# A two-layer attention trunk on one core: the columns and vectors of v's scales made by ScalarE instead of VectorE

## The chip, the core and the metric

The kernel runs on one core of a Trainium2 chip. The core has five engines that are used here: TensorE (PE in the profile; its weight loads are PEld), VectorE (DVE), ScalarE (ACT), GpSimd (POOL) and SyncE (SP), which issues all DMAs. Every engine works through its own list of instructions in order; an instruction that waits holds up everything behind it on its engine. The metric is the device time of one execution in microseconds (us), lower is better. The kernel before took 1829.58 us (median of 3 runs, 1827.2 to 1830.59).

## What is computed

The reference is a trunk of two layers over a sequence of 1024 rows of 1024 numbers, float32, one batch. Each layer adds to x a gated mixer's output through an output matrix:

```python
for i in range(DEPTH):                       # DEPTH = 2
    h = rms_norm(x, norm_g[i])
    if i % 2 == 0:
        o, gate = fox_mixer(h, ...)          # causal attention with a forget gate
        w_out = fox_w_out[0]
    else:
        o, gate = dsw_mixer(h, cos, sin, ...)  # three dilated sliding windows, mixed by softmax
        w_out = dsw_w_out[0]
    x = x + (o * silu(gate)) @ w_out
```

The FoX mixer projects h to q, k, v, gate and a forget logit (16 heads of 64), normalizes q and k, and attends causally with a decay. The dilated mixer (DSW) projects h to q, k, v of three groups (windows 128, 512, 2048 with dilations 1, 4, 16) and a gate, normalizes q and k and rotates a part of them, attends in each group within its window, and mixes the three groups by their log sums.

## The kernel before, in words

**Rounds.** The projections of both layers are worked off in rounds. A round is a pair of heads (FoX: 8 rounds) or a pair of heads and a group (DSW: 24 rounds, first the 8 of group 0, then groups 2 and 1 in turn for each pair of heads). In a round, `project` (line 313) multiplies eight tiles of 128 rows with the round's weights, 384 columns (128 each of k, q, v) and 8 slabs of 128 rows of the weights. Each product is made of three matmuls: activations and weights are both split into a high part and a remainder (`xh`, `xl`; `w[:, 0]`, `w[:, 1]`), and high times high, high times remainder and remainder times high are summed.

**Weights.** A round's weights are loaded as four tiles `raw` of two slabs each (line 253, two buffers), and each slab is split: ACT casts the high part (line 289), then GpSimd or, for slabs 4 and 6, DVE takes the remainder (line 291). `bound` (line 258) takes the largest absolute value of the columns of v on DVE, and `scale` (lines 270 to 281) makes from it a power of two, `vs`, by which v is scaled so that it fits in float16 as two parts. These steps belong to the next round and are put in during the present one by `Flow`, a table of slots that is advanced by four ticks a tile (the offsets in `CFG`: `wload`, `wbound`, `wscale`, `wsplit`).

**v and its scale.** At the start of a round two small instructions make what v needs: `v_tile` (line 462) writes `vs` into column 128 of each of the 8 x 2 blocks of the tile `vt` (128x16 numbers; that column is the row sum's column in the product of probabilities and v), and lines 743 (FoX) and 996 (DSW) multiply the 8 row factors of the norm with `vs` to `vsr` (128x8). Both are `tensor_scalar` instructions of DVE. For each tile, lines 388 (ACT) and 389 (DVE) then write v times `vsr` into `vt` as a high part and a remainder.

**q and k.** For each tile DVE multiplies q and k with the gains out of the projection's PSUM tile `pj` (line 378, to `u`), ACT squares them (383); for each two tiles DVE sums the squares (396, 398), ACT and DVE make the inverse root inside `pj` (416 to 420), DVE applies it to `u` (422, which reads `pj` last), ACT casts a high part to `hl` (424), GpSimd takes the remainder (425), DVE copies the two k blocks in exchanged order (426), and SP transposes `hl` by DMA to `qk_t` (430). In the DSW rounds GpSimd rotates a part of `u` before that (410 to 413). There are three buffers of `pj`, so TensorE cannot begin a tile before the tile three earlier has been read for the last time.

**Attention.** Scores are matmuls of `qk_t` tiles (450); DVE adds the mask or decay and takes the minimum (658, 906), ACT makes the exponentials (492, 907) and casts them (495, 911), GpSimd takes the remainder (498, 912), SP transposes by DMA to `ptt` (499, 913), and TensorE multiplies with `vt` (506 to 508). In group 1, GpSimd also weighs the three groups (936 to 940) and DVE combines them (947 to 955).

**Order.** TensorE's order is as the program is written. The lists of the other engines are ordered by a scheduler at build time, from its own estimate of how long each instruction takes; so moving an instruction to another engine can also change the order around it.

Of the kernel before, what the change touches and what calls it, by code (L numbers as in the profile page):

```python
# [16 lines left out]
AF = mybir.ActivationFunctionType  # L17
ALU = mybir.AluOpType
# [4 lines left out]
P = 128  # L23
# [3 lines left out]
NT = S // P  # L27
# [24 lines left out]
def tile_cols(g, t):  # L52


    if g < 2:
        return slice(t * P, (t + 1) * P, 1)
    a = 2 * P * (t % 4) + t // 4
    return slice(a, a + 2 * 127 + 1, 2)
# [24 lines left out]
def trunk(ctx, tc, ins, out, cfg):  # L83
    nc = tc.nc
# [31 lines left out]
    def lay(shape, dtype, name, tag):  # L116
        return layer["pool"].tile(shape, dtype, name=name, tag=tag, bufs=layer["bufs"][tag])
# [187 lines left out]
    def part(src, i, layer=0):  # L305
        return Weights(src[i], src[i].shape[2], None, layer)

    def project(w, cols):
        n = w.n
        ps = under["ps"] = ps_pj.tile([P, 512], F32, name="pj", tag="pj")  # L310
        for k in range(KT):
            for i, (a, j) in enumerate(((xh, 0), (xh, 1), (xl, 0))):
                nc.tensor.matmul(ps[:, :n], a[:, k, cols], w.slabs[k][:, j, :n], start=(k == 0 and i == 0), stop=(k == KT - 1 and i == 2))  # L313
            if k % 2:
                flow.tick()
        return ps
# [142 lines left out]

    def v_tile(vs):  # L460
        vt = lay([P, NT, 2, 129], F16, name="vt", tag="vt")
        nc.vector.tensor_scalar(vt[:, :, :, 128], vs.unsqueeze(2).broadcast_to([P, NT, 2]), 1.0, None, ALU.mult)  # L462
        return vt

    def gates(src, w, nxt, rows, before=None, after=None):
# [48 lines left out]
    rx = const.tile([P, 3, NT], F32, name="rx")  # L514
# [33 lines left out]
    w = part(w_fgate, 0)  # L548
# [72 lines left out]
    def load_bc(hp, h, es=(0, 1)):  # L621
        for e in es:
            bcs[hp, e, h] = lay([P, 512], F32, name="bc", tag="ga")
            nc.sync.dma_start(bcs[hp, e, h], c_d[2 * hp + e, h * 512 : (h + 1) * 512].partition_broadcast(P))
# [103 lines left out]
    def fox_weights(hp):  # L728
        return Weights(w_fox[hp], 384, slice(256, 384), 0)

    w = gates(w_fgate, w, lambda: fox_weights(0), rx, x_ready, forget_logits)
    for hp in range(NHP):
        w2 = (fox_weights(hp + 1) if hp + 1 < NHP else part(w_fo, 0)).ahead()
        s0 = flow.now
        if hp == 0:
            load_bc(0, 0)
        for h, e, slot in cfg["bc"]:
            if hp + 1 - h < NHP:
                flow.at(s0 + slot, lambda n=hp + 1 - h, h=h, e=e: load_bc(n, h, (e,)))
        kts = []  # L740
        vt = v_tile(w.vs)
        vsr = sm.tile([P, NT], F32, name="vsr", tag="vsr")
        nc.vector.tensor_scalar(vsr, rx[:, 0], w.vs, None, ALU.mult)
        for t in range(NT):
            ps = project(w, tile_cols(0, t))
            if t % 2 == 0:
                hd = heads_begin()
            heads_tile(ps, 0, t, hd, vt, vsr[:, t : t + 1], rx[:, 2, t - 1 : t + 1])
            if t % 2:
                with tc.high_priority(cfg["ph_"]):  # L750

                    turn = heads_pair(0, t - 1, hd)
                    flow.at(flow.now + (6 if hp < NHP - 1 else 4), lambda turn=turn, kts=kts: kts.append(turn()))
                for i in range(2):

                    tt = t - 1 + i
                    fox_tile(hp, tt, kts, vt, s0 + (cfg["due"][tt] if hp < NHP - 1 else 4 * tt + 18))
            if hp == NHP - 1:

                a = max(flow.now + 1, s0 + cfg["due"][t] - 4 * NT + cfg["lpf"] + 9)  # L760
                turn_y(t, 0, [(flow.now + 1, flow.now + 8), (a, a + 7)])
        w = w2
# [4 lines left out]
    rx2 = const.tile([P, 3, 3 * NT], F32, name="rx2")  # L767
# [62 lines left out]
    for h in range(len(PARTS)):  # L830
# [17 lines left out]
        w = w2  # L848
# [26 lines left out]
    w = gates(w_gate, w, lambda: dsw_weights(0), rx2, switch)  # L875
# [116 lines left out]
    for ci, (hp, g) in enumerate(order):  # L992
        w2 = (dsw_weights(ci + 1) if ci + 1 < len(order) else part(w_do, 0)).ahead()
        vt = v_tile(w.vs)
        vsr = sm.tile([P, NT], F32, name="vsr", tag="vsr")
        nc.vector.tensor_scalar(vsr, rx2[:, 0, g * NT : (g + 1) * NT], w.vs, None, ALU.mult)
        qks = [None]
        for t in range(NT):
            if ci == NHP - 1:
                reload_x(t)  # L1000
            ps = project(w, tile_cols(g, t))

            LSD, LPD = cfg["lsd"][max(0, ci - len(order) + 3)]
            if t % 2 == 0:
                hd = heads_begin()
            f = g * NT + t
            heads_tile(ps, g + 1, t, hd, vt, vsr[:, t : t + 1], rx2[:, 2, f - 1 : f + 1])
            if t % 2 == 0:
                continue
            t0 = t - 1  # L1010
            with tc.high_priority(cfg["ph_"]):
                qks = [qks[-1], heads_pair(g + 1, t0, hd)()]
            if g != 1:

                def done(og, ob, g=g, hp=hp, t0=t0):
                    nc.scalar.copy(og[:, :, :, : HD + 1], ob[:, : N2 * (HD + 1)].rearrange("p (i e d) -> p i e d", i=2, e=2))
                    rows = og_d[g // 2, hp].rearrange("(i p) d -> i p d" if g == 0 else "(p i) d -> i p d", p=P)
                    nc.sync.dma_start(rows[t0 : t0 + 2].rearrange("i p d -> p i d"), og.rearrange("p i e d -> p i (e d)"))
                    written.update(((hp, g, t0), (hp, g, t0 + 1)))

                dsw_pair(g, t0, qks, vt, done, lambda: lay([P, 2, 2, 66], F32, name="og", tag="og"), LSD, LPD)
            else:
                cmb = {}

                def get(cmb=cmb):
                    cmb[0] = lay([P, 3, CB, 2, 66], F32, name="cmb", tag="cmb")
                    return cmb[0][:, 0]

                def done(dst, ob, hp=hp, t=t, cmb=cmb):
                    if hp == NHP - 1:  # L1030
                        combine(hp, t, cmb, ob)
                    else:
                        flow.at(flow.now + 1, lambda: combine(hp, t, cmb, ob))

                dsw_pair(g, t0, qks, vt, done, get, LSD, LPD)
                flow.at(flow.now + LSD + 2, lambda hp=hp, t0=t0, cmb=cmb: load_cmb(hp, t0, cmb))
                flow.at(flow.now + LSD + LPD - 5, lambda cmb=cmb: weigh(cmb))
                if hp == NHP - 1:
                    for i in range(2):
                        turn_y(t0 + i, 1, [(flow.now + a + 2 * i, flow.now + b + 2 * i) for a, b in cfg["ty2"]])  # L1040
        w = w2
# [8 lines left out]
    for h in range(len(PARTS)):  # L1050
        w2 = part(w_do, h + 1).ahead() if h < 2 else None
        project_t(h, w, finished)
        w = w2
# [57 lines left out]
```

## Time and profile before

| | |
|---|---|
| median of 3 runs | 1829.58 us (1827.2 to 1830.59) |
| profiled execution: its own time / span | 1830.41 us / 1828.6 us |
| granted TensorE clock | 0.992 of full speed |
| busy: PE, PEld | 1739.1 us (95%), 1638.8 us (90%) |
| busy: DVE, ACT, POOL | 1116.6 us (61%), 999.6 us (55%), 976.9 us (53%) |
| FoX rounds | from about 113 to 500 us |
| DSW rounds, group 0 | from about 758 to 1088 us |
| DSW rounds, groups 2 and 1 | from about 1088 to 1740 us |

The rest are the gates (0 to 113, 662 to 758) and the output matrices (500 to 662, 1740 to the end). A row of a timeline gives the start (us from the span's start), the duration in us, the engine, the line of the kernel, the operation, the tiles written and read, the shape and how many instructions were merged; in brackets, how long the engine was idle before it, and what ended that. SPq is a DMA being issued by SP. A row of the waits gives who waited for what, the sum in us, how often, and the longest.

### The profile page before, as it was taken

The page shows a single profiled execution, that of the slowest core. Times are in us where ns is not written, and L with a number is a line of the kernel's source. Part 1 is how long each engine was busy: PE and PEld are TensorE (multiplying, and loading weights), DVE is VectorE, ACT ScalarE, POOL GpSimd, SP SyncE. Part 2 cuts the span into 40 slices and gives each one's busy share as a digit, 9 for nine tenths or more (in the row PEclk, how much of TensorE's full clock was granted, in tenths as well). Part 3 has the DMA queues.
Part 4 walks back from the last instruction along what each step waited for, and adds up shares of the span by engine and source line. Part 5 has one row for each costly group of instructions (what it writes and reads, how often), then busy time and mean ns, then how long its engine had stood idle before and what let it go on. Part 6 is the DMA issues. An engine that isn't in the chain of part 4 may idle for free.

```text
span 1828.6 us, 38155 instructions
## 1 busy us (share of the span) xinstructions
PE 1739.1 (95%) x13276; PEld 1638.8 (90%) x13276; DVE 1116.6 (61%) x3738; ACT 999.6 (55%) x2632; POOL 976.9 (53%) x1175
## 2 busy tenths in 40 slices
PE   7999999998988989999999999999999999999999
PEld 6999888888876779999999899999998999899877
DVE  8546666666664453465565676666675766667641
ACT  6536666666665455455556565555555555455620
POOL 4215556555654422255565665667676665767530
PEclk9999999999999999999999999999999999999999
DMA  8447999989999754357677696666576766667852
GB/s 285 129 124 139 190 194 181 184 175 170 197 194 205 228 163 130 105 116 142 134 140 148 128 209 140 147 138 151 131 166 140 161 149 129 151 135 183 191 157 85
DMA packets 653190, 290.80 MB, mean 159 GB/s; under 512 B 512306, under 2 KB 616754, under 8 KB 652996
## 3 DMA queue, kind: packets, MB, share of 16 engines
q1 hardware_dynamic: 652996, 288.36, 71.4%
q8 instruction: 104, 1.70, 0.4%
q14 instruction: 90, 0.74, 0.1%
HBM read 126.46 MB, written 37.03 MB: 89 GB/s over the span
## 4 chain that ended last, share of the span: by engine, by line
PE 38%; DMA 14%; DVE 9%; ACT 4%; issue 4%; POOL 3%; SPq 1%; POOLq 0%; DVEq 0%; ACTq 0%
PE pj L313 27%; PE pj L336 7%; DMA raw<-in_w_dsw 6%; DMA qk_t<-hl 3%; PE s L450 2%; DMA ptt<-ph 2%; POOL w L291 1%; DVE w L291 1%; DMA og_d<-og 1%; DVE u L422 1%; DMA cmb<-og_d 1%; DVE p L906 1%; DVE u L378 1%; POOL hl L425 1%; DVE vt L462 1%
## 5 line engine op out<-in xcount | busy, mean ns | idle before, releaser
L313 PE MATMUL pj<-w,xh 128*128 128x384 f32 (+2 forms) x4864 | 1259.7, 341 | 35.2 <-DVE u L422 8.6
L313 PEld LDWEIGHTS pj<-w,xh 128*128 128x128 f32 x4864 | 871.4, 191 | 47.2 <-ACT vt L388 9.6
L313 PE MATMUL pj<-w,xl 128*128 128x384 f32 (+2 forms) x2432 | 816.7, 336 | 1.9 <-DVE xl L530 1.9
L313 PEld LDWEIGHTS pj<-w,xl 128*128 128x128 f32 x2432 | 463.6, 191 | 2.8 <-DVE xl L530 2.8
L291 POOL TENSOR_TENSOR w<-raw,w 128x384 fp32r<-128x384 f32 (+2 forms) x258 | 260.2, 1028 | 231.7 <-ACT w L289 228.5
L498 POOL TENSOR_TENSOR ph<-p,ph 128x512 f16<-128x512 f32 (+3 forms) x176 | 173.6, 1003 | 158.4 <-ACT ph L495 147.4
L289 ACT CAST w<-raw 128x384 fp32r<-128x384 f32 (+2 forms) x352 | 162.8, 501 | 113.8 <-PE pj L336 35.9
L425 POOL TENSOR_TENSOR hl<-u,hl 128x512 f16<-128x512 f32 x128 | 151.3, 1182 | 127.6 <-ACT hl L424 127.6
L912 POOL TENSOR_TENSOR ph<-p,ph 128x768 f16<-128x768 f32 (+2 forms) x96 | 155.4, 1619 | 105.4 <-ACT ph L911 105.4
L383 ACT ACTIVATE sq<-pj 128x256 f32<-128x256 f32 x256 | 97.1, 379 | 202.4 <-DVE u L378 200.4
L450 PE MATMUL s<-qk_t 128*128 128x128 f16 (+1 forms) x1504 | 161.6, 247 | 20.7 <-DMA qk_t<-hl 8.4
L336 PE MATMUL pj<-xh,w 128*128 128x512 f32 x512 | 169.6, 402 | 1.3 <-ACT p L907 1.1
L258 DVE TENSOR_REDUCE vm<-raw 128x1 f32<-128x256 f32 x128 | 53.6, 418 | 163.8 <-DMA raw<-in_w_dsw 117.7
L506 PEld LDWEIGHTS <-ptt 128*128 128x128 f16 x1136 | 103.3, 98 | 49.9 <-issue 27.7
L450 PEld LDWEIGHTS <-qk_t 128*128 128x128 f16 x1504 | 110.2, 98 | 38.7 <-issue 19.0
L389 DVE SCALAR_TENSOR_TENSOR vt<-pj,vsr,vt 128x128 f16<-128x128 f32 x256 | 89.6, 350 | 84.2 <-ACT vt L388 83.9
L424 ACT CAST hl<-u 128x512 f16<-128x512 f32 x128 | 79.1, 618 | 103.5 <-DVE u L422 85.6
L492 ACT ACTIVATE p<-p,acc 128x512 f32<-128x512 f32 (+2 forms) x192 | 109.9, 610 | 39.0 <-DVE acc L658 35.0
L495 ACT CAST ph<-p 128x512 f16<-128x512 f32 (+3 forms) x176 | 89.1, 536 | 66.0 <-DMA ptt<-ph 66.0
L336 PEld LDWEIGHTS pj<-xh,w 128*128 128x128 f32 x512 | 97.2, 190 | 23.4 <-ACT p L907 1.3
L396 DVE TENSOR_REDUCE pj<-sq 128x8 f32<-128x512 f32 x128 | 88.4, 690 | 45.8 <-ACT sq L383 45.8
L907 ACT ACTIVATE p<-p,og 128x128 f32<-128x128 f32 (+1 forms) x256 | 98.0, 441 | 32.2 <-DVE og L906 32.1
(171 smaller groups left out, 2647.0 us busy)
## 6 DMA issues: line engine op xcount, KB each, us to landing
raw<-in_w_dsw SPq DMA_DIRECT2D x96, 384.0 KB, 3.8
raw<-in_w_fox SPq DMA_DIRECT2D x32, 384.0 KB, 3.8
og_d<-og SPq DMA_DIRECT2D x64, 132.0 KB, 3.2
cmb<-og_d SPq DMA_DIRECT2D x64, 132.0 KB, 3.3
bc<-c_d SPq DMA_DIRECT2D x32, 256.0 KB, 4.2
gs_d<-ge SPq DMA_DIRECT2D x32, 192.0 KB, 3.0
xt<-in_xt SPq DMA_DIRECT2D x16, 256.0 KB, 6.1
xrow<-in_x SPq DMA_DIRECT2D x8, 512.0 KB, 6.7
```

What stands on the lines that cost most here:

```text
L289: nc.scalar.copy(w[:, 0, :n], raw[:, k % 2, :n])
L291: eng.tensor_sub(w[:, 1, :n], raw[:, k % 2, :n], w[:, 0, :n].bitcast(F32))
L313: nc.tensor.matmul(ps[:, :n], a[:, k, cols], w.slabs[k][:, j, :n], start=(k == 0 and i == 0), stop=(k == KT - 1 and i == 2))
L336: nc.tensor.matmul(ps[m], w.slabs[k][:, j, m * P : (m + 1) * P], a[:, k, 512 * b : 512 * (b + 1)], start=(k == 0 and x == 0), stop=(k == K ...
L383: nc.scalar.activation(sq[:, t % 2], ps[:, : 4 * HD], AF.Square)
L425: nc.gpsimd.tensor_sub(hl[:, :, :4, 1], u, hl[:, :, :4, 0])
L450: nc.tensor.matmul(s[:, c0 : c0 + cnt * P].rearrange("p (c s) -> p c s", c=cnt), qk[:, i, blk], kk[:, j : j + cnt, e], start=(h == 0), sto ...
L492: nc.scalar.activation(p, p, AF.Exp, bias=acc, scale=-1.0)
L498: (nc.gpsimd if pool_l else nc.vector).tensor_sub(ph[:, e, 1, cols], p, ph[:, e, 0, cols])
L506: nc.tensor.matmul(o[:, e, :], hi, vt[:, j, e, HD:], start=(b == 0), stop=False, skip_group_check=True)
L907: nc.scalar.activation(p[:, e], p[:, e], AF.Exp, bias=acc[:, e : e + 1], scale=-1.0)
L912: nc.gpsimd.tensor_sub(ph[:, 1], st["p"], ph[:, 0])
```

## The change

The two small instructions at the start of each round are issued on ACT: the column of `vt` as a copying ACTIVATE, and `vsr` as a copying ACTIVATE with `vs` as its scale. There are 32 rounds, so 64 instructions leave DVE's list and 64 come into ACT's. What is computed stays the same.

```diff
     def v_tile(vs):
         vt = lay([P, NT, 2, 129], F16, name="vt", tag="vt")
-        nc.vector.tensor_scalar(vt[:, :, :, 128], vs.unsqueeze(2).broadcast_to([P, NT, 2]), 1.0, None, ALU.mult)
+        nc.scalar.activation(vt[:, :, :, 128], vs.unsqueeze(2).broadcast_to([P, NT, 2]), AF.Copy)
         return vt
...
-        nc.vector.tensor_scalar(vsr, rx[:, 0], w.vs, None, ALU.mult)
+        nc.scalar.activation(vsr, rx[:, 0], AF.Copy, scale=w.vs)
...
-        nc.vector.tensor_scalar(vsr, rx2[:, 0, g * NT : (g + 1) * NT], w.vs, None, ALU.mult)
+        nc.scalar.activation(vsr, rx2[:, 0, g * NT : (g + 1) * NT], AF.Copy, scale=w.vs)
```

TensorE's list is the same. The lists of the others differ at these places.

DVE at the start of the DSW round that begins at about 1242 us in the profile before (- before, + the change):

```order
 L281 TENSOR_SCALAR vs<-v_17481 128x1
 L389 SCALAR_TENSOR_TENSOR vt<-pj,vsr,vt 128x2x64
-L462 TENSOR_SCALAR vt<-vs 128x16
-L996 TENSOR_SCALAR vsr<-rx_8351,vs 128x8
 L426 COPY hl<-hl 128x2x256
 L291 TENSOR_TENSOR w<-raw,w 128x384
```

The pair is gone, and the copy into `hl` and slab 6's remainder follow directly on line 389.

ACT at the same place, in the change:

```order
L388 ACTIVATE vt<-pj,vsr 128x2x64
L289 CAST w<-raw 128x384 x2
L462 ACTIVATE vt<-vs 128x16
L996 ACTIVATE vsr<-rx_8351,vs 128x8
L1016 COPY og<-ob 128x4x65
L383 ACTIVATE sq<-pj 128x256
```

The pair stands behind the last two casts of the weights and ahead of the copy of the attention's output (1016) and of the next tile's squares.

DVE some 7 us later in the same round; the same exchange stands in seven DSW rounds, every second one of groups 2 and 1:

```order
 L934 TENSOR_REDUCE mm<-cmb 128x4
 L389 SCALAR_TENSOR_TENSOR vt<-pj,vsr,vt 128x2x64
-L258 TENSOR_REDUCE vm<-raw 128x1
-L378 TENSOR_TENSOR u<-pj,gr 128x256
-L258 TENSOR_REDUCE vm<-raw 128x1
+L258 TENSOR_REDUCE vm<-raw 128x1 x2
+L378 TENSOR_TENSOR u<-pj,gr 128x256
 L419 SCALAR_TENSOR_TENSOR pj<-pj,rs_v 128x8
 L420 SCALAR_TENSOR_TENSOR pj<-pj,rs_y 128x8
```

The product with the gains (378) stood between the two bounds of the next weights, and now stands behind both.

DVE in the last round of group 0, in which x is also read in again (line 988), at about 1050 us in the profile before:

```order
-L389 SCALAR_TENSOR_TENSOR vt<-pj,vsr,vt 128x2x64
-L419 SCALAR_TENSOR_TENSOR pj<-pj,rs_v 128x8
-L258 TENSOR_REDUCE vm<-raw 128x1
+L419 SCALAR_TENSOR_TENSOR pj<-pj,rs_v 128x8
+L389 SCALAR_TENSOR_TENSOR vt<-pj,vsr,vt 128x2x64
 L420 SCALAR_TENSOR_TENSOR pj<-pj,rs_y 128x8
 L988 TENSOR_TENSOR xl<-x_14675,xh 128x4x128
-L378 TENSOR_TENSOR u<-pj,gr 128x256
-L422 TENSOR_TENSOR u<-u,pj 128x512
+L422 TENSOR_TENSOR u<-u,pj 128x512
+L258 TENSOR_REDUCE vm<-raw 128x1
+L378 TENSOR_TENSOR u<-pj,gr 128x256
```

The bound (258) moved from ahead of the inverse root's steps (420, 422) to behind them. In six FoX rounds, further, SP issues one transpose of `ptt` (499) ahead of the transpose of `qk_t` (430) that it followed before, GpSimd has the same exchange (498 ahead of 425), and DVE and ACT exchange neighbours in the same stretch, some 12 us into the round; the starts of these rounds differ only by the pair.

## The prediction

> **What bounds the kernel now.** I read first what TensorE itself waits for, then the stage in which most of that lies, then the two instructions that the change moves. The longest rows of TensorE's waits, over the FoX rounds (113 to 500 us), over group 0 of the DSW rounds (850 to 1040 us) and over groups 2 and 1 (1088 to 1740 us):
>
> ```profile
> PE o L506 <- DMA ptt<-ph: 16.1, 9, 3.4
> ...
> PE s L450 <- DMA qk_t<-hl: 3.0, 3, 1.1
> ...
> PEld pj L313 <- ACT vt L388: 9.6, 7, 1.8
> PE pj L313 <- DVE u L422: 8.6, 8, 1.6
> PE pj L313 <- DVE w L291: 2.2, 4, 0.7
> ```
>
> TensorE sets the time; what can be won is only what it waits, and these are waits for others' chains: in FoX for the transposed probabilities, in group 0 for `qk_t`, in groups 2 and 1 for a free `pj`, about once in every second round (8 waits of 1.08 us on the mean, 7 of them of one kind by the weight loads' row). The question is which of them hang on lines 462, 743 and 996. These instructions, grouped by form:
>
> ```profile
> L462 DVE TENSOR_SCALAR vt<-vs 128x16 f16<-128x16 f32 x32 | 25.5, 796 | 0.1
> L996 DVE TENSOR_SCALAR vsr<-rx,vs 128x8 f32<-128x8 f32 x24 | 17.6, 735 | 0.0
> L743 DVE TENSOR_SCALAR vsr<-rx,vs 128x8 f32<-128x8 f32 x8 | 8.3, 1038 | 0.0
> ```
>
> They are tiny (8 to 16 numbers a lane) and take 0.74 to 1.04 us each on the mean: 51.4 us of DVE in all. The timeline of a round's start shows why, and what stands behind them:
>
> ```profile
> 1240.93 1.29 POOL L425 TENSOR_TENSOR hl<-u,hl 128x512 f16<-128x512 f32 x1 [1.51 <-ACT hl L424]
> 1242.18 1.05 POOL L939 TENSOR_TENSOR cmb<-cmb,wt 128x520 f32<-128x520 f32 x1
> 1242.21 1.08 DVE L462 TENSOR_SCALAR vt<-vs 128x16 f16<-128x16 f32 x1
> 1243.18 1.05 DVE L996 TENSOR_SCALAR vsr<-rx,vs 128x8 f32<-128x8 f32 x1
> 1243.19 2.10 POOL L291 TENSOR_TENSOR w<-raw,w 128x384 fp32r<-128x384 f32 x2
> 1244.14 0.28 DVE L426 COPY hl<-hl 128x512 f16<-128x512 f16 x1
> 1244.48 1.42 SPq L430 DMA_TRANSPOSE qk_t<-hl  x1
> 1246.07 0.39 ACT L383 ACTIVATE sq<-pj 128x256 f32<-128x256 f32 x1 [3.08 <-DVE u L378]
> 1246.95 0.89 SPq L253 DMA_DIRECT2D raw<-in_w_dsw  x2
> ```
>
> Line 462 begins 0.03 us after GpSimd's 939 and ends 0.06 us after it (1243.29 against 1243.23); line 996 ends with GpSimd's next. So each sits out one instruction of GpSimd. Behind them in DVE's list stands the copy 426, whose input was ready at 1242.22; SP's list stands still at the transpose 430 until 426 is done, and the next weights (`raw`, 253) are behind that. What becomes of it 7 us later:
>
> ```profile
> 1250.91 0.42 DVE L258 TENSOR_REDUCE vm<-raw 128x1 f32<-128x256 f32 x1 [1.88 <-DMA raw<-in_w_dsw]
> 1251.25 0.41 DVE L378 TENSOR_TENSOR u<-pj,gr 128x256 f32<-128x256 f32 x1
> 1251.89 0.42 DVE L258 TENSOR_REDUCE vm<-raw 128x1 f32<-128x256 f32 x1 [0.23 <-DMA raw<-in_w_dsw]
> 1252.71 0.69 DVE L422 TENSOR_TENSOR u<-u,pj 128x512 f32<-128x512 f32 x1
> 1253.54 0.59 PE L313 MATMUL pj<-w,xh 128*128 128x384 f32 x2 [1.25 <-DVE u L422]
> ```
>
> DVE's list stands at a bound of the next weights, waiting for `raw`; the inverse root's steps and 422 are behind that, and TensorE waits 1.25 us for the `pj` that 422 frees. So the pair on DVE is at the head of a chain that ends in TensorE's wait: 462, 996, 426, 430, raw, 258, 422. The round 40 us later is a control in the same trace, since there the copy stands ahead of the pair:
>
> ```profile
> 1282.19 0.71 DVE L426 COPY hl<-hl 128x512 f16<-128x512 f16 x1
> 1282.97 1.42 SPq L430 DMA_TRANSPOSE qk_t<-hl  x1
> ```
>
> There the pair delays no transpose. The weight loads' row counts seven waits, and seven is also the number of rounds in which the change makes the exchange of 258 and 378, all of the first kind.
>
> **The change part by part.** *Seven rounds of groups 2 and 1.* With the pair gone, 426 follows 389 and comes to the place where 462 stood. It is a copy that itself can be held by GpSimd (0.71 us in the control against 0.28 free), and 939 has then just begun. I therefore let it end where 462 ended, about 1243.35 instead of 1244.42: 1.07 us earlier, not the 2.1 us that the pair takes. SP comes from 426 to `raw` without a gap that anything else sets, so `raw` lands 1.05 us earlier. Then the order takes a part back: 378 (0.41 us, net some 0.36, as neighbours on DVE overlap: 996 begins 0.11 us before 462 ends), which now uses the wait between the two bounds, stands behind both in the change and ahead of the inverse root. From the second 258 (1251.89) to the end of 422 (1253.40) are 1.51 us now and would be 1.87. The second `raw` at 1250.84, plus 1.87, is 1252.71: 0.7 us earlier. Seven rounds of 0.7 are 4.9; since a wait can't shrink below nothing and some are under the mean of 1.08, I take 4.8 us. Slab 6's remainder (DVE's 291, next behind the copy) also comes earlier, but what TensorE gains there (the row of 2.2 us) only lets it come earlier to the `pj` that ends the chain, so nothing is added for it.
>
> *Group 0.* Two rounds' starts, and the wait that follows the first:
>
> ```profile
> 873.26 1.00 DVE L462 TENSOR_SCALAR vt<-vs 128x16 f16<-128x16 f32 x1
> 875.11 0.28 DVE L426 COPY hl<-hl 128x512 f16<-128x512 f16 x1
> ...
> 895.61 0.56 PE L450 MATMUL s<-qk_t 128*128 128x128 f16 x7 [1.08 <-DMA qk_t<-hl]
> ...
> 914.94 0.20 DVE L462 TENSOR_SCALAR vt<-vs 128x16 f16<-128x16 f32 x1
> 914.94 2.12 POOL L291 TENSOR_TENSOR w<-raw,w 128x384 fp32r<-128x384 f32 x2
> 915.02 0.98 DVE L996 TENSOR_SCALAR vsr<-rx,vs 128x8 f32<-128x8 f32 x1
> 915.91 0.28 DVE L426 COPY hl<-hl 128x512 f16<-128x512 f16 x1
> ```
>
> In the first, 462 takes 1.00 us and the pair holds DVE for 1.85 us until the copy; the copy takes the place of 462 and is done 1.0 us earlier, and the wait of 1.08 us shrinks by that. In the second, 462 slipped in ahead of GpSimd's 291 and only 996 was held; the copy, whose input comes from GpSimd's instruction just before, would be held by the same 291 and ends at 916.1 as now, not at 915.3: 0 to 0.9 us, and I take 0.1, as the copy needs that signal first. Of the 3.0 us of the stage I take 1.2.
>
> *Last round of group 0.* Here the order changes more:
>
> ```profile
> 1054.13 0.42 DVE L258 TENSOR_REDUCE vm<-raw 128x1 f32<-128x256 f32 x1 [2.55 <-DMA raw<-in_w_dsw]
> ...
> 1058.92 0.29 DVE L426 COPY hl<-hl 128x512 f16<-128x512 f16 x1
> ...
> 1063.91 0.84 PE L450 MATMUL s<-qk_t 128*128 128x128 f16 x10 [1.45 <-DMA qk_t<-hl]
> ```
>
> DVE waits 2.55 us at a bound, with the inverse root's last steps behind it; in the change these are done inside the wait. From the bound's end (1054.55) to the copy are 4.4 us now; 420, 422 (0.69 us by its row above) and a split of x leave that stretch, over 1 us of it, and 378 and the reads of scores stay. I take 1.0 us of the 1.45, between 0 and the whole.
>
> *What ACT pays.* The pair has no row on ACT. Nearest by size are:
>
> ```profile
> L937 ACT ACTIVATE wt<-wt 128x12 f32<-128x12 f32 x32 | 6.6, 205 | 6.2 <-POOL wt L936 6.2
> L388 ACT ACTIVATE vt<-pj,vsr 128x128 f16<-128x128 f32 x256 | 91.4, 357 | 0.0
> ```
>
> 0.2 us each by the first (it is nearest in numbers a lane), at most 0.36 by the second: 0.41 us a round, 13 us of ACT in all. It stands ahead of 383, before which ACT was idle 3.08 us in the round shown; that idle time hides it, and if it were gone each round would pay 0.41. The scales were ready when 462 began (1242.21), 3.9 us before 383, so waiting for them adds nothing. I book nothing. The Trainium skill ("ScalarE: Activation LUTs", Rules for kernel authors) speaks against the move: it sends multiplications to VectorE and budgets about 0.3 us for an ACTIVATE. By that page's figure, an estimate, the 64 would cost 20 us of ACT where the rows say 13; and where the page takes VectorE to be the cheaper engine, the rows above (0.74 to 1.04 us on DVE) say otherwise here.
>
> *FoX.* The start of a round:
>
> ```profile
> 192.68 2.20 SPq L430 DMA_TRANSPOSE qk_t<-hl  x1
> ...
> 195.47 1.55 POOL L498 TENSOR_TENSOR ph<-p,ph 128x512 f16<-128x512 f32 x1
> ...
> 198.63 3.46 SPq L499 DMA_TRANSPOSE ptt<-ph  x1
> ```
>
> Here the copy and 430 stand ahead of the pair, so the long waits for `ptt` hang on SP's list and not on the pair. DVE's two remainders (291) come earlier and would hold GpSimd's 498 longer, by 0.5 us if the 1.55 of its row against the 1.05 of 939 is a measure; SP takes its result only at 198.63, 1.6 us after it is done, and hides it. The exchange of transposes lies where TensorE does not wait. I book 0, between 1 us won and 3 us lost (six rounds of 0.5).
>
> The sum is 4.8 + 1.2 + 1.0 = 7.0 us. The profiled execution took 1830.41 us, so 1823.4; it was 0.8 us over the median of the runs, so 1822.6 against 1829.58. About 0.2% (3.7 us) is what a measurement of this kernel can tell from no change.
>
> **The rivals.** *The copy gets through at once.* If 426 reaches DVE before GpSimd takes up its next instruction, as 462 did at 914.94, the whole 2 us of the pair go. Then seven waits vanish but for the exchange (7.0), group 0's too (3.0), the last round's (1.4) and some of the 2.2 us for slabs: 13 us, 1816.5. For it: 914.94. Against it: in the rounds at 1242 and 873 the same place was held, and the copy has to wait for a signal from the engine that it races. The Trainium skill ("SBUF — State Buffer", Who interferes with whom) says that of such a pair whoever issues first holds the port for its whole instruction; by it this rival needs the copy to issue first.
>
> *Nothing moves.* `raw` lands no earlier because the DMA engines, and not SP, set it, or TensorE's wait returns a round later in another place: 0 to 2 us, 1828.5. If only the exchange of 378 then stays, it costs seven times 0.36, 2.5 us. For it: the DMA engines are busy 70% in this stage:
>
> ```profile
> 1088.00:1740.00 652.00, 631.93 (x4685) 611.74 (x4684) 437.83 (x1613) 357.89 (x1064) 424.14 (x582) 1.00 0.70 151
> ```
>
> Against it: `raw` is issued at 1246.95, and the first of the two ends DVE's wait at 1250.91, 4.0 us later; SP's list comes to that issue without another wait, so an earlier 430 makes it earlier.
>
> *ACT becomes the head of the chain.* The pair on ACT delays what it feeds to TensorE: 0.41 us in each of 32 rounds is 13 us, and with half of it hidden 6.5: 1836. It decides where ACT has less than 0.41 us idle between the pair and the next result that TensorE waits for; in the round shown it has 3.08, so it would have to be in rounds whose idle time the earlier 378 uses up. By the ScalarE page's figure (an estimate) its full price would be 20 us and not 13, 1849.6; the rows' price is used.
>
> **How the numbers follow.** The forecast gets 0.47, the copy that gets through 0.17, nothing 0.28, ACT 0.08. The likeliest time is 1822.6. The range reaches down to the second case (1816.5, with half a microsecond to spare) and up to nothing at all, 1829.5. Faster by over 0.2% are the second case, nearly all of the forecast and a little of nothing: 0.63; within 0.2% 0.29; slower 0.08.
>
> **What would show it.** Right, if in the seven rounds 426 ends with the instruction of GpSimd that begins beside it, 430 and `raw` come 1.0 us earlier after the round's start, and the row of TensorE's waits for 422 falls from 8.6 to 3 or 4 us; if group 0's row falls from 3.0 to about 1.8; and if DVE loses some 50 us and ACT gains 13. Wrong, if 426 ends at once (then the waits go nearly to nothing), if `raw` lands when it did, or if 383 or 289 begin later than their inputs on ACT and TensorE waits for them. A FoX part (113 to 500) that is over 2 us longer or shorter would be a mistake of the term that I set to 0.

## The result and the profile after

The changed kernel took 1814.23 us (median of 5 runs, 1813.71 to 1818.97), the kernel before beside it 1830.59 us (1827.2 to 1833.34): a ratio of 0.9919, 95% interval 0.9898 to 0.9939, so 14.8 us faster. Two later comparisons gave 0.9945 (0.9926 to 0.9964) and 0.9942 (0.9927 to 0.9958), that is 10.0 and 10.6 us. The forecast was 7.0. The wait-free kernel below (the pair on DVE in forms that do not wait for GpSimd) was run a second time for its profile, since TensorE had only 0.82 of its clock in the first.

The profiled execution after took 1818.5 us, its span 1816.7 us. The busy line of its page, and the groups of the two that now stand in the pair's place on DVE (copy and slab remainder) and of the moved instructions:

```profile
PE 1737.0 (96%) x13276; PEld 1641.7 (90%) x13276; DVE 1093.3 (60%) x3674; ACT 1011.0 (56%) x2696; POOL 973.5 (54%) x1175
```

```profile
L291 DVE TENSOR_TENSOR w<-raw,w 128x384 fp32r<-128x384 f32 x86 | 78.4, 914 | 9.8 <-ACT w L289 8.8 <-DMA out<-xr 0.8
L426 DVE COPY hl<-hl 128x512 f16<-128x512 f16 x128 | 68.9, 538 | 78.0 <-POOL hl L425 77.7 <-DMA y_d<-y 0.2
...
L462 ACT ACTIVATE vt<-vs 128x16 f16<-128x16 f32 x32 | 8.9, 277 | 0.3 <-DVE vs L281 0.3
L996 ACT ACTIVATE vsr<-rx,vs 128x8 f32<-128x8 f32 x24 | 6.9, 289 | 0.0
L743 ACT ACTIVATE vsr<-rx,vs 128x8 f32<-128x8 f32 x8 | 2.3, 290 | 0.0
```

On ACT the pair costs 0.28 and 0.29 us, 18.1 us in all. DVE lost 51.4 us of work but is only 23.3 us less busy, mainly because the waits for GpSimd go over to its neighbours: the copy 426 and the remainder 291 take 10.7 and 8.6 us longer than before (58.2 and 69.8 us there), which is 19.3 of the 28.1 us between the two numbers.

What TensorE waits for after, over the FoX rounds, group 0, and groups 2 and 1 (sum in us, how often, longest):

```profile
PE o L506 <- DMA ptt<-ph: 13.2, 10, 2.9
...
PE s L450 <- DMA qk_t<-hl: 1.1, 2, 0.9
...
PE pj L313 <- DVE u L422: 6.0, 7, 1.6
...
PE pj L313 <- DVE vt L389: 2.2, 3, 0.8
...
PE pj L313 <- POOL w L291: 0.4, 1, 0.4
```

FoX has lost 2.9 us of waits for `ptt`, but is 0.8 us shorter only, as TensorE's waits for DVE's 658 grew there from 8.3 to 10.4 us. The row for 422 fell less than forecast (8.6 to 6.0), while rows of groups 2 and 1 that the forecast had left alone are gone or nearly so: the remainder 291 on DVE (2.2 us) and, of the three further rows of before that follow, the first and the third:

```profile
PE s L450 <- DMA qk_t<-hl: 2.1, 5, 0.8
PE pj L313 <- DVE vt L389: 1.8, 3, 1.0
PE pj L313 <- POOL w L291: 1.2, 2, 0.8
```

The windows of group 0 and of groups 2 and 1 after (us, busy time of PE, PEld, DVE, ACT, POOL, clock, DMA share) are 3.3 and 9 us shorter than before (330 and 652 us) at the same clock:

```profile
758.30:1085.00 326.70, 321.67 (x2526) 314.23 (x2525) 198.51 (x676) 191.73 (x527) 191.67 (x234) 0.99 0.71 145
1085.00:1728.00 643.00, 629.56 (x4683) 611.71 (x4683) 428.19 (x1581) 362.49 (x1094) 422.87 (x582) 1.00 0.70 154
```

The round of the prediction once more, in a selection of rows. First rows of before that the prediction left out, from the scale's last step (281) to the reads of scores (906) and what follows from them:

```profile
1241.85 0.15 DVE L281 TENSOR_SCALAR vs<-v 128x1 int32<-128x1 int32 x1
1244.34 1.36 DVE L291 TENSOR_TENSOR w<-raw,w 128x384 fp32r<-128x384 f32 x1
1245.63 0.41 DVE L378 TENSOR_TENSOR u<-pj,gr 128x256 f32<-128x256 f32 x1
1245.76 0.45 PE L313 MATMUL pj<-w,xh 128*128 128x384 f32 x1 [0.71 <-DVE w L291]
1245.96 0.28 DVE L906 CUSTOM_DVE_ANT_0 p<-s,band 128x128 f32<-128x128 f32 x1
...
1249.43 1.66 POOL L912 TENSOR_TENSOR ph<-p,ph 128x768 f16<-128x768 f32 x1 [0.76 <-ACT ph L911]
...
1254.05 2.31 SPq L253 DMA_DIRECT2D raw<-in_w_dsw  x2
...
1259.21 1.46 SPq L430 DMA_TRANSPOSE qk_t<-hl  x1
```

The same place after:

```profile
1238.62 0.15 DVE L281 TENSOR_SCALAR vs<-v 128x1 int32<-128x1 int32 x1
1239.01 1.13 DVE L426 COPY hl<-hl 128x512 f16<-128x512 f16 x1
...
1240.07 1.36 DVE L291 TENSOR_TENSOR w<-raw,w 128x384 fp32r<-128x384 f32 x1
...
1241.35 0.41 DVE L378 TENSOR_TENSOR u<-pj,gr 128x256 f32<-128x256 f32 x1
1241.69 0.27 DVE L906 CUSTOM_DVE_ANT_0 p<-s,band 128x128 f32<-128x128 f32 x1
...
1242.67 0.88 SPq L253 DMA_DIRECT2D raw<-in_w_dsw  x2
...
1245.16 1.66 POOL L912 TENSOR_TENSOR ph<-p,ph 128x768 f16<-128x768 f32 x1 [0.57 <-ACT ph L911]
...
1249.77 2.28 SPq L253 DMA_DIRECT2D raw<-in_w_dsw  x2
1250.08 0.59 PE L313 MATMUL pj<-w,xh 128*128 128x384 f32 x2 [1.62 <-DVE u L422]
...
1254.46 1.58 SPq L430 DMA_TRANSPOSE qk_t<-hl  x1
```

The copy is held by GpSimd and takes 1.13 us, as forecast, and the first `raw` is issued 3.90 us after the end of 281 (1238.77) in place of 4.95 (1242.00). But two more things moved. DVE is through with the whole group (pair, copy, remainder) earlier: it comes to the last tile's 378 2.58 us after 281 and not 3.63, and to the reads of scores at 2.92 us and not 3.96. And the second transpose comes at 15.7 us and not 17.2. TensorE's wait for 422 did not shrink in this round: it stood 0.71 us for 291 and 1.25 us for 422 before, and 1.62 us for 422 alone after. Which of the moves pays is what the experiments had to tell.

### The profile page after: what moved, and what is told of

The parts are those of the page before. It is cut to its first block, busy times and chain, and to the rows that moved or that the text cites. A ratio compares the mean times of both kernels' runs of the same rounds, so it can differ in the third digit from the quotient of the medians.

```text
span 1816.7 us, 38150 instructions
## 1 busy us (share of the span) xinstructions
PE 1737.0 (96%) x13276; PEld 1641.7 (90%) x13276; DVE 1093.3 (60%) x3674; ACT 1011.0 (56%) x2696; POOL 973.5 (54%) x1175
## 4 chain that ended last, share of the span: by engine, by line
PE 45%; DMA 12%; DVE 6%; ACT 4%; issue 3%; POOL 3%; SPq 1%; DVEq 0%; POOLq 0%; ACTq 0%
PE pj L313 33%; PE pj L336 7%; DMA raw<-in_w_dsw 5%; PE s L450 2%; DMA qk_t<-hl 2%; DMA ptt<-ph 2%; DMA og_d<-og 1%; POOL hl L425 1%; POOL w L291 1%; DMA cmb<-og_d 1%; DVE w L291 1%; DVE hl L426 1%; DVE u L422 1%; PE ob L506 1%; DVE p L906 1%
## 5 line engine op out<-in xcount | busy, mean ns | idle before, releaser
L450 PE MATMUL s<-qk_t 128*128 128x128 f16 (+1 forms) x1504 | 162.0, 248 | 19.2 <-DVE acc L658 10.4
L378 DVE TENSOR_TENSOR u<-pj,gr 128x256 f32<-128x256 f32 x256 | 106.4, 416 | 18.4 <-PE pj L313 18.3
```

The costliest lines, as they stand in the source:

```text
L378: nc.vector.tensor_mul(u[:, t % 2].rearrange("p (a b) d -> p a b d", a=2), ps[:, : 4 * HD].rearrange("p (a b d) -> p a b d", a=2, b=2), gr ...
L450: nc.tensor.matmul(s[:, c0 : c0 + cnt * P].rearrange("p (c s) -> p c s", c=cnt), qk[:, i, blk], kk[:, j : j + cnt, e], start=(h == 0), sto ...
```

## The experiments

The forecast's theory was the copy's chain: 426, 430, `raw`, 258, 422. The first rivals were a general relief of DVE, and the order that the scheduler made.

**Parts of the change.** Column only:

```diff
-        nc.vector.tensor_scalar(vt[:, :, :, 128], vs.unsqueeze(2).broadcast_to([P, NT, 2]), 1.0, None, ALU.mult)
+        nc.scalar.activation(vt[:, :, :, 128], vs.unsqueeze(2).broadcast_to([P, NT, 2]), AF.Copy)
```

> Only the column (line 462) goes to ACT; the row factors vsr (743, 996) stay on DVE and take 462's place. Theory (the pair waits for GpSimd's port ahead of the copy 426 and of slab 6's remainder): the remaining instruction sits out one instruction of GpSimd as each of the two did, so line 996 keeps about 0.7 us on the mean, one instruction's wait goes per round, and the time falls by 5 to 9 us of the 15. Rival (each instruction that DVE loses counts alike, wherever it stands): half of the 15 too, 7 us, but spread over FoX as well. Rival (the order made by the scheduler brings the gain): this kernel already has the exchange of 258 and 378, so 12 to 15 us.

Measured 0.9972 (0.9957 to 0.9987), 5.1 us faster; 996 then takes 1.00 us on the mean, so it does sit out the wait that 462 had. In its profile groups 2 and 1 are as short as with both moved (638.5 us), and group 0 is as long as before (328.9). Its DVE list, by the trace, does not have the exchange of 258 and 378 that its expectation took it to have, so it does not test the order; the wait-free kernel below does.

Both instructions, but in the FoX rounds only, and then in the DSW rounds only (in the other rounds the lines of before):

> Both instructions go to ACT in the 8 FoX rounds alone; the DSW rounds keep them on DVE. Theory (the gain is made at the starts of DSW rounds): 0, from 2 us faster to 2 us slower, and the stretch from 758 us to the end as before. Rival (relief of DVE as such): a quarter of the 15 us, 4 us faster, in the stretch from 113 to 500 us. Rival (new order in FoX costs or brings something by itself): over 2 us either way in that stretch.

> Both instructions go to ACT in the 24 DSW rounds alone; the FoX rounds keep them on DVE. Theory: the whole gain, 12 to 17 us faster, with the row of waits for 422 near 6 us, and the rows for slab remainders (291) and for qk_t in groups 2 and 1 nearly gone. Rival (relief of DVE as such): three quarters, 11 us. If the new order in FoX brings part of it: under 11 us.

FoX only: 0.9998 (0.9984 to 1.0012). DSW only: 0.9962 (0.9944 to 0.9979), 6.9 us, where 12 to 17 were expected. The gain is made in the DSW rounds; relief of DVE as such would have shown in FoX.

The changed and the unchanged kernel again, to see what two executions differ by:

> The changed kernel itself, beside the kernel before on one chip once more. The sum of the two parts measured so far (FoX only 0, DSW only 7 us faster) says 4 to 10 us faster; if the 15 us of the first comparison belong to the change and not to the runs that were compared, 12 to 17.

> The kernel before itself, for a second profile of it. If its waits in groups 2 and 1 are fixed by the program, the rows for 422, for slab remainders (291) and for qk_t come within 1 us of 8.6, 3.4 and 2.1; if they move by several us from one execution to the next, the 15 us of the first comparison hold some of that.

After: 0.9945, as told above. Before: 1824.05 us, with 6.3 us at 422, 3.3 at 291 and 1.8 at `qk_t`: the waits move by up to 2.3 us from one execution to the next. The FoX part, which by the run above the change does not shorten, was 387.1 and 384.5 us in the two profiles of before, and 386.3, 381.7 and 384.6 in three of after. Some of the first comparison's 15 us is of that kind.

**The wait or the order.** The pair stays on DVE and in its place, in forms that do not wait for GpSimd:

```diff
-        nc.vector.tensor_scalar(vt[:, :, :, 128], vs.unsqueeze(2).broadcast_to([P, NT, 2]), 1.0, None, ALU.mult)
+        nc.vector.tensor_reduce(vt[:, :, :, 128], vs.unsqueeze(2).unsqueeze(3).broadcast_to([P, NT, 2, 1]), AX.X, ALU.max)
...
-        nc.vector.tensor_scalar(vsr, rx2[:, 0, g * NT : (g + 1) * NT], w.vs, None, ALU.mult)
+        nc.vector.tensor_scalar(vsr, rx2[:, 0, g * NT : (g + 1) * NT], w.vs, None, ALU.mult, ALU.max, accum_out=w.vm[:, 0:1])
```

> The pair stays on DVE and the lists of DVE, GpSimd and SP keep their order of before (two exchanges of the pair with a neighbour apart); only the form changes: the column is a reduction over an axis of one number, and the row factors are a tensor_scalar that also writes out its accumulator. Theory (what cost was the wait for the shared port and not DVE's own work or the order): both rows fall from 0.74 to 1.04 us to about 0.2 us, DVE loses about 35 us or what others then wait, and the time falls by 12 to 18 us, as much as with ACT or 2 us more, since the exchange of 258 and 378 (booked at seven times 0.36) isn't made. Rival (the scheduler's new order brings the gain): within 2 us of before. Rival (the pair's place on DVE costs, whatever its form): 0 to 4 us faster.

> The pair on DVE in forms that do not wait for GpSimd, for a profile at the usual clock. Theory: the rows of slab remainders and of qk_t in groups 2 and 1 are gone as in the changed kernel, 462 and 996 take 0.2 to 0.3 us each, and the copy 426 behind them is held by GpSimd as in the changed kernel.

Measured 0.9964 (0.9947 to 0.9980), 6.6 us, less than expected (line 743 has the same new form). The groups of its second profile:

```profile
L462 DVE TENSOR_REDUCE vt<-vs 128x16 f16<-128x16 f32 x32 | 6.9, 217 | 0.1
L996 DVE TENSOR_SCALAR_CACHE_REDUCE vsr<-rx,vs 128x8 f32<-128x8 f32 x24 | 5.0, 209 | 0.0
L996 DVE DVE_READ_ACCUMULATOR vsr<-rx,vs 128x1 f32 x24 | 1.9, 80 | 0.0
```

With 0.2 us each, and with the lists of DVE and GpSimd in the order of before, most of the gain is there: it was the wait for GpSimd, and neither the order nor ACT. This kernel does not make the exchange of 258 and 378 either. The times cannot tell what that is worth: groups 2 and 1 take 643.3 us here and 640.9 to 643.2 in three profiles after.

**The price on ACT, and a dose.** The changed kernel with both instructions issued twice on ACT, and the kernel before with both issued twice on DVE:

> The changed kernel with each of the two instructions issued twice on ACT (the second writes the same numbers). By their rows after the change (277 and 289 ns) that is 0.57 us more of ACT in each of 32 rounds, 18 us in all. Theory (ACT's idle time at the round's start hides the pair): 0 to 3 us slower than the changed kernel. Rival (ACT's part is on the path, and what was gained is the port's wait less that): 9 to 18 us slower than it.

> The kernel before with each of the two instructions issued twice on DVE (the second writes the same numbers). Theory (they wait for GpSimd ahead of the copy and the remainder): two more waits of 0.74 to 1.04 us at the head of each round, DVE up by some 40 to 50 us, and the time up by as much as the change takes off or more, 7 to 15 us slower than before, with longer rows for 422, 291 and qk_t. Rival (the gain came from the scheduler's new order, not from the waits): 0 to 2 us.

Twice on ACT: 0.9955 (0.9940 to 0.9970), beside 0.9945 (0.9926 to 0.9964) of the changed kernel on the same chip: 1.8 us more by the two ratios, and no more than 8 by the far ends of their intervals, for 18 us of ACT. It hides most of them. Twice on DVE: 1.0036 (1.0023 to 1.0050), 6.6 us slower, just under the expected 7. The second copies were held less (645 and 481 ns on the mean of all), and the wait that grew is this one, over groups 2 and 1:

```profile
PE s L450 <- DMA qk_t<-hl: 5.8, 8, 1.8
```

**What stands behind the pair.** Now the pair was left on DVE, waits and all, and only moved behind the copy, then behind the slab remainder too, by tying its place to these instructions in the DSW rounds. Only the order in DVE's list is set by that; `copies` holds the copies 426 as they were issued, and `copies[-2]` is the one that stood behind the pair:

```diff
-        vt = v_tile(w.vs)
+        with tc.issue_after(copies[-2]): vt = v_tile(w.vs)
...
-        nc.vector.tensor_scalar(vsr, rx2[:, 0, g * NT : (g + 1) * NT], w.vs, None, ALU.mult)
+        with tc.issue_after(copies[-2]): nc.vector.tensor_scalar(vsr, rx2[:, 0, g * NT : (g + 1) * NT], w.vs, None, ALU.mult)
```

> The pair stays on DVE as tensor_scalar, but in the DSW rounds its place is behind the copy 426: copy, pair, slab remainder 291 in place of pair, copy, remainder. Theory (two paths out of the round's start, the transpose and raw behind the copy, and the slab behind the remainder): the rows for 422 and qk_t shrink to 5 and under 1 us, the row for 291 stays at 2 to 3.4 us, and the time falls by 4 to 7 us, about two thirds of the changed kernel's 10. The step of the forecast that nothing is added for the slab says instead: all of the changed kernel's gain, 8 to 10 us.

> As the last, with the pair behind the slab remainder as well: copy, remainder, pair. DVE has the same work and the same waits for GpSimd as before, only later. Theory (it counts what stands behind the pair, not what the pair costs): the rows for 291 and qk_t nearly go, and the time falls as far as with ACT, 7 to 12 us. Rival (the time that DVE loses to the port counts, wherever it stands): 0 to 3 us faster.

Measured 0.9993 (0.9976 to 1.0010) and 1.0006 (0.9993 to 1.0019): nothing that can be told from no change, and at most 4.4 us by the interval of the first. Here the forecast's theory fell, and mine of two paths with it. In the first of the two the waits for 422 went down as the forecast had it, but those for the transposed q and k came up from 2.1 us:

```profile
PE s L450 <- DMA qk_t<-hl: 4.7, 6, 1.5
PE pj L313 <- DVE u L422: 2.6, 5, 0.6
```

The round in the second:

```profile
1235.88 0.15 DVE L281 TENSOR_SCALAR vs<-v 128x1 int32<-128x1 int32 x1
1236.27 1.13 DVE L426 COPY hl<-hl 128x512 f16<-128x512 f16 x1
...
1238.61 1.01 DVE L462 TENSOR_SCALAR vt<-vs 128x16 f16<-128x16 f32 x1
1239.51 0.78 DVE L996 TENSOR_SCALAR vsr<-rx,vs 128x8 f32<-128x8 f32 x1
1239.90 0.89 SPq L253 DMA_DIRECT2D raw<-in_w_dsw  x2
1240.20 0.41 DVE L378 TENSOR_TENSOR u<-pj,gr 128x256 f32<-128x256 f32 x1
1240.54 0.27 DVE L906 CUSTOM_DVE_ANT_0 p<-s,band 128x128 f32<-128x128 f32 x1
...
1244.01 1.66 POOL L912 TENSOR_TENSOR ph<-p,ph 128x768 f16<-128x768 f32 x1 [0.76 <-ACT ph L911]
...
1248.65 2.30 SPq L253 DMA_DIRECT2D raw<-in_w_dsw  x2
...
1253.34 1.45 SPq L430 DMA_TRANSPOSE qk_t<-hl  x1
```

Copy and first `raw` are as early as after (3.87 us from the end of 281, 1236.03), but the reads of scores come at 4.51 us. From there 907 and 911 feed GpSimd's 912, which begins at 7.98 us (before 7.43, after 6.39). In all three timelines GpSimd was idle ahead of 912 until 911 released it, and then went without a gap through 939, four remainders, 940 and 425. The four remainders free the buffers of the next `raw`, and that issue comes at 12.6 us (before 12.05, after 11.0). The second transpose needs 425, and comes at 17.3 us (17.2, 15.7). So the row for 422 fell to 5.6 us, and the waits for `qk_t` grew to 6.5:

```profile
PE s L450 <- DMA qk_t<-hl: 6.5, 7, 1.6
PE pj L313 <- DVE u L422: 5.6, 7, 1.4
```

The second theory was then: the moment at which DVE reaches 378 and the reads of scores sets the round's end. Four kernels for it. The pair behind the last tile's 389, and so behind 378 and the reads (as above, with 389's instruction in place of the copy's); the same in the rounds of group 2 alone; the changed kernel itself; and the changed kernel with two more small `tensor_scalar` on DVE between remainder and 378, whose output nobody reads (`rems` holds DVE's remainders 291):

```diff
+        with tc.issue_after(copies[-2]), tc.issue_after(rems[-1]): nc.vector.tensor_scalar(w.vm, rx2[:, 0, :4], w.vs, None, ALU.mult); nc.vector.tensor_scalar(w.vm, rx2[:, 0, :4], w.vs, None, ALU.mult)
```

> The pair stays on DVE as tensor_scalar, but in the DSW rounds its place is behind the last tile's line 389, where DVE waits for raw anyway. Second theory (what counts is when DVE comes to the last tile's 378 and the reads of scores behind the group of pair, copy and remainder): that group shrinks from 3.78 to about 2.74 us as in the changed kernel, and the time falls by 7 to 11 us with the pair still on DVE. Rival (any place on DVE costs, since the pair waits for the port there or the instructions around it do): 0 to 3 us faster, as with the pair behind copy and remainder.

> The pair on DVE; in the rounds of group 2 its place is behind the last tile's 389 (there both had 0.2 us each, 0.42 in all), in the other DSW rounds it stands behind the copy or ahead of it as before. Second theory (the group's length ahead of 378 counts, eight rounds of 1.04 us, and what e11 lost came from the rounds of group 1): 5 to 10 us faster than before, without a row of waits for 389 over 2.5 us. Rival (any place on DVE costs as much): 0 to 2 us faster.

> The changed kernel with two more small tensor_scalar of 128x4 on DVE in each DSW round, behind copy and remainder and ahead of the last tile's 378; their output (the tile of the bounds, done with by then) is read by nobody, and the pair stays on ACT. Second theory: the group grows from 2.74 to 4.3 us, and the whole gain is lost, 0 to 3 us of it left. If instead it counts that the pair itself is off DVE, or when vsr is ready: the gain stays, 7 to 13 us faster than before.

> The changed kernel once more, beside the other three on one chip: 7 to 13 us faster than before.

Made long again, the group loses the whole gain though the pair is on ACT: 1.0006 (0.9993 to 1.0019), beside 0.9942 (0.9927 to 0.9958) of the changed kernel. Behind 389 in all DSW rounds: 0.9995 (0.9981 to 1.0009), a miss; in the rounds of group 1 the pair came so late that the next tile's `vt` (389) waited for it, which a row that grew from 1.8 us shows:

```profile
PE pj L313 <- DVE vt L389: 5.8, 4, 2.3
```

In the rounds of group 2 alone: 0.9965 (0.9953 to 0.9976), 6.4 us faster, with every instruction still on DVE. There the pair falls where DVE waits for `raw` and GpSimd is idle:

```profile
1245.75 0.20 DVE L462 TENSOR_SCALAR vt<-vs 128x16 f16<-128x16 f32 x1
1245.83 0.23 DVE L996 TENSOR_SCALAR vsr<-rx,vs 128x8 f32<-128x8 f32 x1
1246.25 1.66 POOL L912 TENSOR_TENSOR ph<-p,ph 128x768 f16<-128x768 f32 x1 [0.55 <-ACT ph L911]
1247.83 0.42 DVE L258 TENSOR_REDUCE vm<-raw 128x1 f32<-128x256 f32 x1 [1.77 <-DMA raw<-in_w_dsw]
```

Last, 378 or the reads of scores. The remainder is tied behind the last tile's 378 (`mul`) in the changed kernel, and in the kernel before with the pair on DVE between remainder and reads:

```diff
+        ); gi > 0 and t == NT - 1 and tc.add_manual_dep([i for e, i in rems if e is nc.vector][-1], mul.ins.name, mybir.DependencyInfo(mybir.DependencyClass.NoSync, mybir.DependencyReason.DATA), reason="last tile first")
```

> The changed kernel with the last tile's 378 ahead of the slab remainder 291 in the DSW rounds: 378 comes 1.36 us earlier, the reads of scores (906) come when they came. If the way to TensorE's waits runs through 378 (383, 396, 398, 422): 5 to 10 us faster than the changed kernel. If it runs through the reads of scores (906, 907, 911, 912 and GpSimd's remainders behind it): within 3 us of the changed kernel.

> The pair on DVE in the DSW rounds in the order copy, last tile's 378, slab remainder, pair, reads of scores. 378 comes as early as in the fastest kernel so far, the reads of scores as late as in the run with the pair behind copy and remainder. If 378 sets the end: 8 to 15 us faster than before. If the reads of scores set it (906, or the sum 396 that stands behind them): within 3 us of before. In between, both count.

The first is the fastest kernel of all: 1807.73 us, 0.9910 (0.9894 to 0.9925), beside 0.9942 for the changed kernel. By its expectation that spoke for 378, but the second, with 378 as early and the reads late, is no faster than before: 1.0016 (0.9998 to 1.0034). In its rounds of group 2, 378 is 2.3 us earlier than before, and yet 912 begins at 7.7 us and 425 at 14.9 (before 7.4 and 14.6, after 6.4 and 13.6). But neither kernel is clean. The first had not separated them as I meant: its reads come 0.33 us earlier too (2.58 us after 281), and in the rounds of group 1 the scale's last step 281 comes 1.1 to 1.4 us earlier (3.09 us after TensorE's product for the scale, line 270, against 4.22 to 4.46 after). In the second, in the rounds of group 1, the reads come 0.5 us later after 281 than before, and in all of these rounds but the first GpSimd's 912 has fallen behind two more remainders. The second's waits:

```profile
PE s L450 <- DMA qk_t<-hl: 13.5, 9, 3.1
PE pj L313 <- DVE u L422: 5.4, 7, 1.2
```

The profiles of all these kernels together, worked out from their traces, one execution each: the mean over six rounds of group 2 (the second to the seventh of eight), in us after the end of 281, of the first issue of `raw`, of 378 and of the first read of scores (906), and the length of groups 2 and 1 between the same two instructions of TensorE.

| kernel | `raw` | 378 | 906 | groups 2 and 1 |
|---|---|---|---|---|
| before (twice), FoX only | 4.9 | 3.62 | 3.96 | 652.0, 646.9, 651.1 |
| twice on DVE | 4.88 | 4.38 | 4.71 | 655.7 |
| behind copy | 3.83 | 3.62 | 3.96 | 647.7 |
| behind copy and remainder | 3.84 | 4.18 | 4.51 | 649.0 |
| after, group made long | 3.84 | 4.18 | 4.51 | 652.3 |
| 378 first, pair on DVE | 3.86 | 1.29 | 4.18 | 654.2 |
| after (three times) | 3.85 | 2.58 | 2.91 | 643.2, 641.9, 640.9 |
| DSW only, twice on ACT | 3.9 | 2.58 | 2.92 | 640.1, 639.8 |
| wait-free on DVE | 3.84 | 2.58 | 2.91 | 643.3 |
| behind 389, group 2 only | 3.87 | 2.58 | 2.92 | 640.9 |
| behind 389, all DSW rounds | 3.91 | 2.58 | 2.91 | 645.1 |
| column only | 3.93 | 2.65 | 2.99 | 638.5 |
| after, 378 first | 3.91 | 1.29 | 2.58 | 640.1 |

An early `raw` without early reads wins nothing that can be told (four kernels, but only behind copy do the reads come when they came before; in the other three they are later). An early 378 without early reads won nothing in the one kernel that has it, with what was said of it above. Every kernel that has the reads at 2.6 to 3.0 us is at 645.1 us or under (the longest of them is the one with new waits for `vt`), every one that has them at 3.96 or later at 646.9 or over; the kernel before alone spans 646.9 to 652.0 in its profiles. The sum 396 follows the first read 0.76 to 0.77 us later in every row, so the two are not separated. The last row comes from an execution of 1813.96 us, the longest of its five (median 1807.73), and so does not show the 6 us that this kernel gained beyond the changed one. What brings them stays open; GpSimd's list has changed in that kernel too.

## Why the prediction was off

**The bound** was read rightly: TensorE's waits, at the starts of the DSW rounds, through a pair that sits out GpSimd's instructions. Leaving the waits away with the pair still on DVE gives most of the gain.

**The step that failed** is the term of the seven rounds, 4.8 us: it took the 0.7 us by which 422 comes earlier for the gain of a round. The links up to 422 are right one by one. The copy is held by 939 and ends 1.05 us earlier, `raw` is issued 1.05 us earlier, and 422 ends 10.8 us after 281 on the mean of the seven rounds, where it was 11.4 (three profiles after, three with the pair in its place), 0.64 us earlier. But in these rounds TensorE is mainly stopped at three places, as its waits in the traces show: 2 to 4 us after 281 for remainders of slabs, some 11 us for 422, and some 21 us for the second transpose. "SP comes from 426 to `raw`" and on to 422 was taken to set the end, and "nothing is added" for what stands next on DVE. In the kernel behind copy 422 ends at 10.7 us, as forecast or better, and TensorE's waits for it fall to 2.6 us (8.6 and 6.3 in the two profiles of before). TensorE then stands for the second transpose instead (4.7 us in place of 2.1 and 1.8), and the kernel is 1.3 us faster, at most 4.4 by its interval, where 4.8 were booked.

What pays is that DVE reaches the last tile's 378 and the reads of scores earlier, by 1.05 us in seven rounds and 0.5 us in the first of group 2, 7.9 us in all; with the reads GpSimd's 912 and the second transpose come earlier too. Groups 2 and 1 shrank by 8.0 us (means of the three lengths of before and after in the table, 650.0 and 642.0). The two numbers need not agree so well: with its reads 0.55 us later than before, the kernel behind copy and remainder is slower by 1.1 us only (1.3 faster to 3.5 slower), presumably because its copy and remainder are early. That it is the reads and not 378 rests on the timelines, where 911 releases 912, and on one kernel that is not clean.

The control at 1282 is a round of group 1. The kernel that moves the pair in the rounds of group 2 alone is as short in groups 2 and 1 as the changed one (640.9 and 642.0 us), so the rounds of group 1 have no visible part in the gain.

**The exchange of 378** was priced at 0.36 us in seven rounds, and the traces bear the price out: from the start of the second bound to the end of 422 are 1.50 us before and in the wait-free kernel, and 1.88 us after. No time of a whole kernel shows it, which fits a round whose end is not set by 422.

**Group 0 and its last round**: forecast 2.2 us, measured 2.2 (328.5 before, of 329.9, 327.4 and 328.2; 326.3 after, of 326.6, 326.4 and 325.9). That the numbers agree is partly luck: 1.0 us was booked on the wait for `qk_t` in the last round, 1.45 us in the profile before, but this wait was 2.0 and 2.2 us in the other two with the pair in its place, and 0.66, 2.35 and 1.87 us in the three after.

So 8.0 + 2.2 = 10.2 us belong to the change, as the two later comparisons have it (10.0, 10.6), and not 7.0; what the first comparison has beyond that lies in stages whose length changes from one execution to the next, and no run ties it to the change. That it is chance is inferred and not shown.

**ACT 0**: right as far as the runs can tell; most of twice the pair is hidden too. The row taken for its price (205 ns) was too low: 277 to 290 ns. Here the Trainium skill's 0.3 us an ACTIVATE ("ScalarE: Activation LUTs", Rules for kernel authors) was nearer, and its advice to leave multiplications to VectorE does not hold where VectorE has to wait for GpSimd.

**FoX 0**: right, 0.9998 (0.9984 to 1.0012).

**The rivals**: the copy does not get through at once (1.13 us against 0.28 free), though the time came out near that rival's; ACT is not the head of a chain. Something did move, but the mechanism of that rival, a wait of TensorE that returns in another place, is what the kernel behind copy shows. "DVE loses some 50 us" was wrong by half, mainly because a wait for GpSimd passes on to the next instruction that can wait for it, as shown above.

## What to carry to other kernels

An instruction that waits in an in-order list delays all that stands behind it, so work out when the engine reaches each of the later chains and price the one that ends last, not the first one that you can follow. The place of a small instruction counts: here each of the two took 0.2 us where DVE waited for `raw` and GpSimd was idle, and about 1 us where GpSimd had just begun, ahead of work that TensorE came to wait for. Before an experiment is read as a proof for one of two paths, look in its profile whether the other one moved too.

## What the runs showed of the hardware

DVE's wait depends on the form of the instruction and, between 8 and 16 numbers a lane, not on its size: the `tensor_scalar` of 128x8 in the DSW rounds took 0.22 to 1.06 us, the 128x16 one 0.19 to 1.17; as a reduction over an axis of one number, or with its accumulator written out, the same work took 0.20 to 0.23 us in every round (and 0.08 for the accumulator's read). The Trainium skill ("SBUF — State Buffer", Who interferes with whom) names both forms as free of contention for the port that DVE shares with GpSimd, and these rows agree. On ACT a 128x8 and a 128x16 ACTIVATE took the same, 0.29 and 0.28 us.
